# Part of the attention matrix transposed by TensorE instead of by DMA

## The chip, the cores and the metric

The kernel runs on one core of one Trainium2 chip. The core has a matrix engine (TensorE, PE in the profile, with its weight loads listed as PEld), three elementwise engines (VectorE or DVE, ScalarE or ACT, GpSimd or POOL), a queue engine (SyncE or SP) that issues most transfers, and 16 DMA engines. The metric is the time of one execution on the device in microseconds, as the median of several runs.

## What is computed

One transformer block over a sequence of 2048 rows of 1024 float32 values:

```python
u   = rms_norm(h, norm1_w);  proj = u @ w_in        # [diff q,k,v | sb q,k,v]
y_diff = diff_attention(dq, dk, dv, lam, rel_bias)  # 4 heads, softmax
# stick breaking, 8 heads, no softmax, strictly causal:
z = q @ k.T * scale
log_1mb = where(mask, log_sigmoid(-z), 0)
rem = cumsum(log_1mb, axis=keys, reverse=True) - log_1mb
a = where(mask, exp(log_sigmoid(z) + rem), 0);  y_sb = a @ v
h = h + concat(rms_norm(y_diff), rms_norm(y_sb)) @ w_out
h = h + (silu(u2 @ w_gate) * (u2 @ w_up)) @ w_down  # u2 = rms_norm(h, norm2_w)
```

The change concerns the product of the stick-breaking weights `a` with `v`. TensorE contracts over partitions, so `a`, which is made with queries on partitions and keys along the row, has to be transposed first: blocks of 128 queries by 128 keys, keys onto partitions.

To keep float32 accuracy with 16-bit operands, a float32 value is split into a high float16 part and a low one (the value less the high part). A product then takes three matmuls: high by high, high by low, low by high.

## The kernel before

The work falls into eight head groups and then the output projection and the feed-forward part. Groups 0 to 3 are one differential head each (`diff_attn`); groups 4 to 7 are two stick-breaking heads each (`sb_attn`). While a group's attention runs, the projection of the next group is issued in small pieces between its units: `advance` follows the share of the group's work that is done. So TensorE has projection matmuls (L341) to do in between. Groups 4 to 6 are the "turned" ones, whose q and k come out of the projection already transposed (`proj_turned`, `turned_out`).

Within a group of `sb_attn` the loop runs over 16 query blocks `i`, over key ranges `b` of up to 1024 keys from the last to the first, and over the two heads `m`. One turn of it is a unit. For `i` from 0 to 7 there is one range of 128 to 1024 keys; for `i` from 8 to 15 there is a range of 128 to 1024 keys and then one of 1024. That gives 48 units in a group. Of these, 16 have 512 keys or fewer: eight at the start of the group (`i` from 0 to 3) and eight in its middle (`b` = 1, `i` from 8 to 11), where they alternate with units of 1024.

`stage_a` makes a unit's weights. For each chunk of up to 512 keys TensorE writes the scores into a PSUM tile `sc` (L506, and L508 for the mask). ACT applies two sigmoids to it (L618, L619), DVE runs the product scan along the row (L621), and DVE, or POOL for the first half of a wide unit, multiplies (L622). The result stands in the float32 tile `be`. `split_t` then makes the high part on ACT (a cast in the helper on L89), the low part on POOL (a subtraction in the helper on L98), both into a 16-bit tile `s16`, and one DMA transpose on SP's queue (L460) turns both parts into the tile `aT`. After a delay of `lag` units (7, and 5 in group 6) `stage_b` issues the matmuls with `v` (L517).

Tiles come from rings: four `sc` tiles in PSUM, nine `z4` tiles (each unit takes two, `be` and `om`), three `s16` tiles, six `aT` tiles. In groups 4 and 5 a counter `wide` sends some units to borrowed tiles for `s16` and `aT` (two of five, and one of four). A new tile waits until the last reader of the one that it replaces is done.

Every engine works through its own queue in a fixed order, which is set when the program is built: a planner orders the instructions by priorities (`PRI`, with `at` for `stage_a` above the rest and `pm` for the projection below) and by its own estimate of when they are ready. Inside `tc.issue_after(x)`, instructions on x's engine are put behind x. `pick` gives an operation to the engine with the lower sum of booked costs, `note` books a cost, and `level` resets the sums at every fourth query block.

Of the kernel before, what the change touches and what calls it, by code (L numbers as in the profile page):

```python
# [11 lines left out]
F32 = mybir.dt.float32  # L12
F16 = mybir.dt.float16
# [3 lines left out]
ALU = mybir.AluOpType  # L17
# [4 lines left out]
S, D, P = 2048, 1024, 128  # L22
# [16 lines left out]
QB, KB, ZB, AB, SB, PD = 4, 7, 9, 6, 3, 5  # L39
# [20 lines left out]
def block(tc, a, out):  # L60
    nc = tc.nc
    PE, ACT, DVE, POOL, SP = nc.tensor, nc.scalar, nc.vector, nc.gpsimd, nc.sync
    top = ExitStack()
    with top:
# [8 lines left out]
        def note(e, ns):  # L73
            load[e] += ns * KW[e]
# [6 lines left out]
        def level():  # L81
            for k in load:
                load[k] = 0.0

        def to16(dst, src, n, engines="ADP", psum=False):
            cost = {"A": 0.84 * n + 110, "D": (1.05 if psum else 0.53) * n + 70, "P": 1.1 * n + 80}
            e = pick(**{k: cost[k] for k in engines})
            if e == "A":
                ACT.copy(dst, src)  # L89
            elif e == "D":  # L90
                DVE.tensor_copy(dst, src)
            else:
                POOL.tensor_scalar(dst, src, 1.0, 0.0, op0=ALU.mult, op1=ALU.add)

        def tt(dst, a_, b_, op, n, engines="DP"):
            cost = {"D": 1.15 * n + 70, "P": 2.45 * n + 80}
            e = pick(**{k: cost[k] for k in engines})
            (DVE if e == "D" else POOL).tensor_tensor(dst, a_, b_, op)  # L98

        def pri(k):  # L100
            def deco(f):
                @functools.wraps(f)
                def g(*args):
                    with tc.high_priority(PRI[k]) if PRI[k] else nullcontext():
                        return f(*args)
                return g
            return deco

        def nm(s):
            uid[0] += 1  # L110
            return f"{s}{uid[0]}"
# [5 lines left out]
        id32 = cp.tile([P, P], F32, name="id32")  # L117
# [138 lines left out]
        with ExitStack() as ph1:  # L256
            sp = ph1.enter_context(tc.tile_pool(name="sp", bufs=2))
            ps = ph1.enter_context(tc.tile_pool(name="ps", bufs=2, space=PSUM))
# [4 lines left out]
            def z4():  # L263
                return zp.tile([P, 1028], F32, tag="z4", bufs=ZB, name=nm("z4"))
# [64 lines left out]
            def turned(g):  # L329
                return 4 <= g < NG - 1  # L330
# [117 lines left out]
            @pri("spl")  # L448
            def split_t(src, n, he="ADP", le="DP", wide=None):
                if wide is not None and wide % 5 in (1, 3):  # L450
                    s16 = pp.tile([P, 4, 256], F32, tag="raw", name=nm("s16"))[:].rearrange("p t n -> p (t n)").bitcast(F16)
                else:
                    s16 = s16p.tile([P, 2048], F16, tag="s16", bufs=SB, name=nm("s16"))
                to16(s16[:, :n], src, n, he)
                tt(s16[:, n : 2 * n], src, s16[:, :n], ALU.subtract, n, le)
                if wide is not None and wide % 4 == 3:
                    aT = pp.tile([P, 4, 4, 2, 64], F16, tag="st", name=nm("aT"))[:].rearrange("p c t s e -> p (c t) (s e)")
                else:
                    aT = sp.tile([P, 16, P], F16, tag="aT", bufs=AB, name=nm("aT"))
                SP.dma_start_transpose(aT[:, : 2 * n // P, :], s16[:, : 2 * n])  # L460
                return aT
# [36 lines left out]
            def fq(g, i):  # L498
                k = 2 if g == NG - 1 else 4
                return (i % k, k)  # L500

            @pri("sc")
            def score_chunk(G, sc, i, q, m, w, cut=False, turned=False):
                terms = ((m, 0), (2 + m, 0), (m, 1)) if turned else ((2 + m, m), (m, m))
                for o, (a_, b_) in enumerate(terms):
                    last = PE.matmul(sc[:, : 128 * w].rearrange("p (t n) -> p t n", n=P), lhsT=G["q"][i // 4][:, a_, i % 4, :], rhs=G["k"][q][:, b_, 0:w, :], start=o == 0, stop=o == len(terms) - 1)  # L506
                if cut:
                    last = PE.matmul(sc[:, 128 * w - P : 128 * w], lhsT=idb[:], rhs=tri[:], start=False, stop=True, skip_group_check=True)  # L508
                return last.ins
# [85 lines left out]
            def sb_attn(g, G):  # L595
                last = {}
                front = []
                wide = [0]
                lag = PD + 2 if g < NG - 2 else PD

                @pri("at")
                def stage_a(i, m, b):
                    L = (i + 1) * 128
                    n = min(1024, L - 1024 * b)
                    be, om = z4(), z4()
                    if b == i // 8:
                        DVE.memset(om[:, n : n + 1], 8192.0)
                    else:
                        DVE.tensor_copy(om[:, n : n + 1], last[m][:, 0:1])
                    last[m] = om  # L610
                    for c in range((n - 1) // 512, -1, -1):
                        lo, hi = 512 * c, min(512 * c + 512, n)
                        w = hi - lo
                        sc = ps.tile([P, 512], F32, tag="sc", bufs=4, name=nm("sc"))
                        front.append(score_chunk(G, sc, i, 2 * b + c, m, w // P, b == i // 8 and hi == n, turned(g)))
                        aside = c == 1 and turned(g)
                        beta = be[:, lo:hi] if aside else sc[:, :w]
                        ACT.activation(om[:, lo:hi], sc[:, :w], AF.Sigmoid, scale=G["nkz"][:])  # L618
                        ACT.activation(beta, sc[:, :w], AF.Sigmoid, scale=G["kz"][:])  # L619
                        ov = om[:, lo:hi][:, ::-1]  # L620
                        DVE.tensor_tensor_scan(ov, ov, sc[:, :w], om[:, hi : hi + 1], op0=ALU.mult, op1=ALU.bypass)  # L621
                        (POOL if aside else DVE).tensor_tensor(be[:, lo:hi], beta, om[:, lo + 1 : hi + 1], ALU.mult)  # L622
                        note("A", 1.7 * w + 400)
                        note("D", 2.1 * w + 150)
                        note("P" if aside else "D", (1.65 if aside else 1.05) * w + 100)
                    wide[0] += 1
                    return n, split_t(be[:, :n], n, "A", "P", wide[0] if g < NG - 2 else None)

                ypd = {}

                def stage_b(i, m, b, n, aT):
                    with tc.issue_after(front[-1]):
                        stage_c(i, m, b, n, aT)

                def stage_c(i, m, b, n, aT):
                    r, k = fq(g, i)
                    if i // k not in ypd:
                        ypd[i // k] = ps.tile([P, 512], F32, tag="yp", name=nm("yp"))
                    yp = ypd[i // k]
                    pv(G, yp, P * r + 64 * m, aT, b, n, 128 * m, 64, r == 0 and m == 0 and b == i // 8, r == k - 1 and m == 1 and b == 0)  # L640
                    if m == 1 and b == 0 and r == k - 1:
                        finish(g, G, i, k, yp)
                        G["fin"] = i + 1

                pend = []
                done = 0
                for i in range(NT):
                    if i % 4 == 0:
                        level()
                    for b in range(i // 8, -1, -1):  # L650
                        for m in range(2):
                            n, aT = stage_a(i, m, b)
                            pend.append((i, m, b, n, aT))
                            if len(pend) > lag:
                                stage_b(*pend.pop(0))
                            done += n // P + CS
                            yield done / (272 + 48 * CS), (i + 1 if b == 0 and m == 1 else i)
                for u in pend:
                    stage_b(*u)

# [212 lines left out]
        with ExitStack() as ph2:  # L873
# [23 lines left out]
            turn = [0]  # L897
# [400 lines left out]
```

## Time and profile before

| | us |
|---|---|
| median of 3 runs (2699.47 to 2701.21) | 2699.54 |
| the profiled execution, whole | 2702.93 |
| its span, first to last instruction | 2701.0 |
| stick-breaking groups 4 to 6 in it | about 612 to 1100 |
| DVE busy, whole span | 1959.8 (73%) |
| PE busy, whole span | 2508.6 (93%) |

The profile is one execution. Busy time of an engine is the union of its instructions' times; matmuls are pipelined, so four that take 0.27 us each can be done 0.6 us after the first began. A row of a group gives line, engine, operation, output and inputs by the program's names, shapes, count, busy time, mean time of one in ns, and after the bar the idle time of the engine before these instructions and what ended it. A row of a timeline gives start, length, engine and line, and in brackets the idle time before it and what ended that. A row of a window gives from-to, length, then the busy time of each engine with its count of instructions, the granted TensorE clock as a share of full speed, the DMA share and the rate in GB/s. A wait reads "who waited <- for what: total us, times, longest".

### The profile page before, as it was taken

To read this page: it belongs to the slowest core of one execution; us is meant where nothing else is said; L and a number is where in the kernel's file an instruction comes from. 1 tells how busy PE (TensorE), PEld (TensorE's weight loads), DVE (VectorE), ACT (ScalarE), POOL (GpSimd) and SP (SyncE) were. 2 spreads that over 40 slices of the span, in tenths; PEclk is the share of its full clock that TensorE was granted. 3 is DMA by queue.
4 is the path that set the end of the run, shared out by engine and by line. 5 is a ranking of instruction groups with operands and counts; after the bars stand their busy time and mean duration, and the time that the engine had idled before them with its cause. 6 is when DMAs were issued, how large, how long until landed. Compare 5 with 4: busy or idle time off the path is not lost. (4 is left out here: it accounts for less than half of the span.)

```text
span 2701.0 us, 50505 instructions
## 1 busy us (share of the span) xinstructions
PE 2508.6 (93%) x19628; PEld 1507.6 (56%) x19628; DVE 1959.8 (73%) x3712; ACT 1344.7 (50%) x2487; POOL 1517.8 (56%) x1097
## 2 busy tenths in 40 slices
PE   7998989899988989889999999999999999999999
PEld 4655656577776776567774444444444444444444
DVE  6898879899989889887866877778685543433434
ACT  4665656567978878765634534435352112111121
POOL 2578767768767767545665755665564332322323
PEclk9999999999999999999999999999999999999999
DMA  6778697768989989997996566565748744635532
GB/s 221 211 163 184 143 200 172 172 145 183 195 175 185 178 166 206 208 205 203 230 317 232 211 232 219 207 239 183 253 171 330 304 159 157 234 132 184 202 110 94
DMA packets 619584, 534.40 MB, mean 198 GB/s; under 512 B 480640, under 2 KB 548224, under 8 KB 609104
## 3 DMA queue, kind: packets, MB, share of 16 engines
q1 hardware_dynamic: 617520, 529.09, 70.1%
q8 instruction: 154, 2.52, 0.4%
q0 software_dynamic: 512, 1.36, 0.2%
q14 instruction: 86, 0.70, 0.1%
q10 hardware_dynamic: 1312, 0.72, 0.1%
HBM read 261.08 MB, written 147.32 MB: 151 GB/s over the span
## 5 line engine op out<-in xcount | busy, mean ns | idle before, releaser
L98 POOL TENSOR_TENSOR s<-z,s 128x1024 f16<-128x1024 f32 (+7 forms) x288 | 471.5, 1646 | 141.8 <-ACT s L89 118.2
L506 PE MATMUL sc<-kT,qT 128*128 128x512 f16 (+3 forms) x1520 | 382.7, 354 | 51.1 <-DVE z L622 18.6
L1104 PE MATMUL pd<-wd,act 128*128 128x512 f16 x1764 | 392.8, 380 | 5.3 <-DVE cu L1038 4.7
L621 DVE TENSOR_TENSOR_SCAN z<-z,sc 128x512 f32<-128x512 f32 (+3 forms) x320 | 352.8, 1112 | 56.5 <-ACT sc L619 34.6
L325 PE MATMUL pj<-w,xt 128*128 128x384 f16 x1920 | 354.6, 333 | 17.1 <-ACT raw L374 5.8
L1004 PEld LDWEIGHTS <-wu 128*128 128x128 f16 x1848 | 181.9, 98 | 224.6 <-issue 12.8
L1004 PEld LDWEIGHTS <-wg 128*128 128x128 f16 x1848 | 181.3, 98 | 222.9 <-issue 9.3
L517 PE MATMUL yp<-v,aT 128*128 128x64 f16 (+1 forms) x4896 | 271.2, 205 | 36.9 <-DMA aT<-s 35.7
L517 PEld LDWEIGHTS <-aT 128*128 128x128 f16 x4896 | 239.1, 100 | 114.4 <-DMA aT<-s 46.7
L98 POOL TENSOR_TENSOR act<-cg,act 128x512 f16<-128x512 f32 x109 | 150.7, 1393 | 259.4 <-ACT act L1063 259.4
L1104 PEld LDWEIGHTS <-act 128*128 128x128 f16 x1764 | 172.9, 98 | 213.5 <-issue 7.2
L325 PEld LDWEIGHTS <-xt 128*128 128x128 f16 x1920 | 187.8, 99 | 147.2 <-issue 23.4
L89 ACT CAST s<-z 128x128 f16<-128x128 f32 (+7 forms) x215 | 173.3, 810 | 135.9 <-DMA aT<-s 44.6
L98 POOL TENSOR_TENSOR stages<-stages 128x512 f32<-128x512 f32 x97 | 171.4, 1767 | 116.5 <-DVE wg L220 42.2
L618 ACT ACTIVATE z<-sc,c 128x512 f32<-128x512 f32 (+3 forms) x320 | 211.2, 665 | 24.4 <-PE sc L506 12.4
L98 POOL TENSOR_TENSOR hs<-hs,cu 128x512 f32<-128x512 f32 x102 | 133.6, 1317 | 159.3 <-DVE hs L1110 59.7
L506 PEld LDWEIGHTS <-qT 128*128 128x128 f16 x1520 | 128.8, 99 | 119.7 <-issue 23.9
L831 PE MATMUL po<-wo,mt 128*128 128x256 f16 x1536 | 182.4, 279 | 12.6 <-DVE xf L834 8.6
L1063 ACT CAST act<-cg 128x512 f16<-128x512 f32 x126 | 76.7, 616 | 231.1 <-DVE cg L1069 192.7
L1110 DVE SCALAR_TENSOR_TENSOR hs<-pd,c,hs 128x512 f32<-128x512 f32 x144 | 106.0, 747 | 115.0 <-PE pd L1104 105.3
L341 PE MATMUL pj<-xt,w 128*128 128x128 f16 x2304 | 177.4, 222 | 6.2 <-DVE v L363 5.2
L1004 PE MATMUL pm<-X,wu 128*128 128x512 f16 x792 | 179.8, 381 | 2.1 <-ACT cg L1049 1.7
(254 smaller groups left out, 4812.3 us busy)
## 6 DMA issues: line engine op xcount, KB each, us to landing
xt<-xs SPq DMA_DIRECT2D x112, 512.0 KB, 4.5
hs<-hd SPq DMA_DIRECT2D x72, 512.0 KB, 4.5
hd<-hs SPq DMA_DIRECT2D x56, 512.0 KB, 5.9
split<-wg SPq DMA_DIRECT2D x11, 1792.0 KB, 6.9
split<-wu SPq DMA_DIRECT2D x11, 1792.0 KB, 6.7
split<-wd SPq DMA_DIRECT2D x11, 1792.0 KB, 6.8
wg<-split SPq DMA_DIRECT2D x11, 1792.0 KB, 7.5
wd<-split SPq DMA_DIRECT2D x11, 1792.0 KB, 9.0
```

Of the source, the lines that this page charges most:

```text
L89: ACT.copy(dst, src)
L98: (DVE if e == "D" else POOL).tensor_tensor(dst, a_, b_, op)
L325: PE.matmul(pj[:, :384], lhsT=xv[:, xi, kt, :], rhs=G["w"][:, wi, kt, :], start=n == 0, stop=n == 23)
L341: PE.matmul(o, lhsT=x_ if c == 2 else w_, rhs=w_ if c == 2 else x_, start=n == 0, stop=n == 23)
L506: last = PE.matmul(sc[:, : 128 * w].rearrange("p (t n) -> p t n", n=P), lhsT=G["q"][i // 4][:, a_, i % 4, :], rhs=G["k"][q][:, b_, 0:w, :] ...
L517: PE.matmul(yp[:, y0 : y0 + wd], lhsT=aT[:, a_, :], rhs=v[:, v_ : v_ + wd], start=start and j == 0 and q == 0, stop=stop and j == nb - 1 a ...
L618: ACT.activation(om[:, lo:hi], sc[:, :w], AF.Sigmoid, scale=G["nkz"][:])
L621: DVE.tensor_tensor_scan(ov, ov, sc[:, :w], om[:, hi : hi + 1], op0=ALU.mult, op1=ALU.bypass)
L831: PE.matmul(po[:, sl], lhsT=mt[:, kt, P * xi : P * xi + P], rhs=wos[2 * h + n][wi][:, kt, :], start=q == 0, stop=q == 23)
L1004: PE.matmul(ps_[:].rearrange("p (t n) -> p t n", n=P), lhsT=wv[:, wo, wi, 128 * kt : 128 * kt + 128], rhs=X[xo][:, :, xi, kt, :], start=st ...
L1104: PE.matmul(po[:], lhsT=act[:, ao, xi, 128 * j : 128 * j + 128], rhs=W["d"][:, wo, wi, :], start=start and u == 0 and q == 0, stop=u == nu ...
L1110: DVE.scalar_tensor_tensor(dst, po[:], kd[:], src, op0=ALU.mult, op1=ALU.add)
```

## The change

In groups 4 to 6 a unit of at most 512 keys no longer goes through `split_t`. `stage_a` hands on its float32 tile `be`, and three units later `turn` is called for it, behind the last score matmul issued so far. `turn` takes one `sc` tile of PSUM, transposes each block of 128 keys in float32 on TensorE (a matmul with the identity `id32`), copies the result as float16 into the high half of an `aT` tile on ACT, and subtracts that from the PSUM tile on DVE into the low half. Units above 512 keys keep the DMA transpose; the counter `wide` counts only these now. `note` books the new ACT and DVE costs.

```diff
+                    if direct(n):
+                        return n, be
                     wide[0] += 1
                     return n, split_t(be[:, :n], n, "A", "P", wide[0] if g < NG - 2 else None)
+
+                def direct(n):
+                    return turned(g) and n <= 512
+
+                @pri("spl")
+                def turn(be, n):
+                    nb = n // P
+                    tr = ps.tile([P, 512], F32, tag="sc", bufs=4, name=nm("at"))
+                    for j in range(nb):
+                        PE.transpose(tr[:, P * j : P * j + P], be[:, P * j : P * j + P], id32[:])
+                    aT = sp.tile([P, 16, P], F16, tag="aT", bufs=AB, name=nm("aT"))
+                    src = tr[:, :n].rearrange("p (c n) -> p c n", n=P)
+                    ACT.copy(aT[:, :nb, :], src)
+                    DVE.tensor_tensor(aT[:, nb : 2 * nb, :], src, aT[:, :nb, :], ALU.subtract)
+                    note("A", 0.84 * n + 110)
+                    note("D", 1.15 * n + 70)
+                    return aT
+
+                def turn_due(n):
+                    u = pend[-n] if len(pend) >= n else None
+                    if u is not None and direct(u[3]):
+                        with tc.issue_after(front[-1]):
+                            u[4] = turn(u[4], u[3])
...
-                            pend.append((i, m, b, n, aT))
+                            pend.append([i, m, b, n, aT])
+                            turn_due(4)
...
+                for n in range(min(3, len(pend)), 0, -1):
+                    turn_due(n)
                 for u in pend:
                     stage_b(*u)
```

## Prediction

> **What bounds the kernel now.** The page comes first, for the span, then the busy time of each engine in stretches of the stage that the change touches, then that stage's waits. All threshold talk below uses 0.2% (5.4 us), about what a measurement of this kernel tells from no change.
>
> ```profile
> span 2701.0 us, 50505 instructions
> ...
> PE 2508.6 (93%) x19628; PEld 1507.6 (56%) x19628; DVE 1959.8 (73%) x3712; ACT 1344.7 (50%) x2487; POOL 1517.8 (56%) x1097
> ```
>
> The 73% of DVE is a mean over unlike stages. Cut into the stretches of groups 4 to 6:
>
> ```profile
> core 0: us, PE busy (x) PEld busy (x) DVE busy (x) ACT busy (x) POOL busy (x), PEclk, DMA share, GB/s
> 612.00:638.00 26.00, 25.04 (x392) 22.36 (x390) 22.98 (x48) 20.12 (x53) 18.67 (x20) 1.00 0.80 172
> 638.00:666.00 28.00, 23.52 (x348) 18.64 (x347) 27.55 (x57) 22.24 (x43) 23.50 (x15) 1.00 0.84 171
> 666.00:707.00 41.00, 36.32 (x559) 28.32 (x558) 38.18 (x61) 35.90 (x66) 31.27 (x25) 1.00 1.09 208
> 707.00:766.00 59.00, 55.17 (x898) 44.28 (x896) 56.37 (x87) 55.30 (x93) 46.79 (x34) 1.00 0.98 184
> 766.00:790.00 24.00, 21.29 (x335) 18.15 (x333) 17.90 (x41) 16.90 (x38) 13.56 (x15) 0.93 0.90 163
> 790.00:826.00 36.00, 30.58 (x463) 24.85 (x462) 31.61 (x62) 26.97 (x52) 25.95 (x17) 1.00 0.79 167
> 826.00:866.00 40.00, 35.45 (x554) 28.11 (x550) 38.17 (x62) 32.77 (x58) 28.49 (x23) 1.00 1.05 209
> 866.00:926.00 60.00, 56.06 (x912) 44.93 (x909) 57.29 (x92) 56.63 (x97) 49.47 (x35) 1.00 1.01 186
> 926.00:948.00 22.00, 19.22 (x292) 16.20 (x290) 17.30 (x37) 15.92 (x36) 11.14 (x13) 0.92 0.87 161
> 948.00:980.00 32.00, 25.49 (x385) 20.48 (x383) 25.16 (x53) 22.39 (x42) 23.55 (x17) 0.95 0.89 179
> 980.00:1030.00 50.00, 46.23 (x733) 38.61 (x730) 44.22 (x73) 38.00 (x70) 28.82 (x24) 0.97 0.81 155
> 1030.00:1100.00 70.00, 62.86 (x663) 39.64 (x661) 65.87 (x114) 58.90 (x104) 55.01 (x38) 1.00 1.02 229
> sum 488.00, PE 437.23 PEld 344.55 DVE 442.61 ACT 402.03 POOL 356.24; mean PE 36.44 PEld 28.71 DVE 36.88 ACT 33.50 POOL 29.69
> ```
>
> Each group has four stretches: its start (612, 766, 926; the first eight small units), a stretch of larger units, its middle (666, 826, 980; the other eight small units between units of 1024), and the rest. DVE is busy 442.6 of 488 us (90.7%), PE 437.2. In the middles of groups 4 and 5 DVE has 93 and 95%, so DVE sets the pace there. The starts are different: in the second and third DVE is at 75 and 79%, and nothing is full. The waits say why.
>
> ```profile
> ACT s L89 <- DMA aT<-s: 20.1, 13, 3.0
> ...
> PE sc L506 <- DVE z L622: 13.4, 19, 1.6
> ...
> DVE z L621 <- ACT sc L619: 11.7, 18, 2.7
> DVE z L621 <- ACT z L619: 11.2, 9, 4.0
> ...
> PE yp L517 <- DMA aT<-s: 10.0, 11, 2.1
> ```
>
> ACT waits 20.1 us until a transpose has left its `s16` tile, and PE 10.0 us for a transposed tile. At the start of group 5, in the timelines of ACT, DVE and PE:
>
> ```profile
> 772.65 0.30 ACT L89 CAST s<-z 128x128 f16<-128x128 f32 x1 [2.88 <-DMA aT<-s]
> 780.23 0.82 ACT L89 CAST s<-z 128x256 f16<-128x256 f32 x2 [3.04 <-DMA aT<-s]
> 773.90 1.01 DVE L621 TENSOR_TENSOR_SCAN z<-z,sc 128x384 f32<-128x384 f32 x1 [1.85 <-ACT sc L619]
> 782.22 1.28 DVE L621 TENSOR_TENSOR_SCAN z<-z,sc 128x512 f32<-128x512 f32 x1 [2.69 <-ACT sc L619]
> 772.67 1.29 PE L517 MATMUL yp<-v,aT 128*128 128x64 f16 x24 [2.15 <-DMA aT<-s]
> 773.77 2.00 PE L341 MATMUL pj<-xt,w 128*128 128x128 f16 x17
> ```
>
> ACT stands behind a small unit's cast, the next unit's sigmoids stand behind ACT, and DVE loses 1.85 and 2.69 us. PE waits 2.15 us for a unit of 24 matmuls (8 blocks by 3, a wide one of group 4), and runs slowly afterwards (17 matmuls in 2.00 us).
>
> **The change part by part.** In each of the six small-unit stretches eight units change, two of each of 128, 256, 384 and 512 keys: 20 blocks. In all 48 units, 120 blocks. Durations:
>
> ```profile
> 665.68 0.61 PE L488 MATMUL yp<-id,y 128*128 128x128 f32 x4
> L683 DVE TENSOR_TENSOR xt<-xtr,xt 128x512 f16<-128x512 f32 x32 | 21.1, 681 | 4.2 <-ACT xt L682 4.2
> L682 ACT CAST xt<-xtr 128x512 f16<-128x512 f32 x32 | 17.7, 586 | 7.3 <-PE xtr L664 6.7 <-ACT raw L374 0.5
> L622 DVE TENSOR_TENSOR z<-sc,z 128x384 f32<-128x384 f32 x12 | 6.7, 555 | 0.5
> L622 DVE TENSOR_TENSOR z<-sc,z 128x256 f32<-128x256 f32 x12 | 5.0, 420 | 1.0 <-POOL s L98 0.5
> L622 DVE TENSOR_TENSOR z<-sc,z 128x128 f32<-128x128 f32 x14 | 3.9, 282 | 0.3
> L89 ACT CAST s<-z 128x512 f16<-128x512 f32 x12 | 7.4, 631 | 0.7 <-DMA aT<-s 0.4 <-DVE z L607 0.3
> L98 POOL TENSOR_TENSOR s<-z,s 128x512 f16<-128x512 f32 x12 | 13.9, 1161 | 1.2 <-ACT s L89 1.2
> L460 SPq DMA_TRANSPOSE aT<-s x288: 1167/1556/5872, 113.7 to 1358.9; - x144
> L362 DVE TENSOR_SCALAR kT<-pj 128x256 f16<-128x256 f32 x20 | 8.3, 413 | 0.0
> L362 DVE TENSOR_SCALAR v<-pj 128x256 f16<-128x256 f32 x15 | 6.1, 408 | 0.6 <-PE pj L341 0.5
> L349 ACT ACTIVATE qT<-pj,half 128x256 f16<-128x256 f32 x42 | 21.8, 519 | 11.2 <-PE pj L341 7.9 <-DVE qT L350 3.2
> ```
>
> *DVE, added.* The subtraction out of PSUM is L683 at 512 keys; shorter ones are taken from L622, which also reads PSUM. Per stretch 2 x (0.282 + 0.420 + 0.555 + 0.681) = 3.88 us, in all 23.3.
>
> *DVE, moved.* The booked DVE cost pushes `pick` towards ACT. Two ACT instructions of L349 come with two picks, so the 42 there mean 42 picks, of which DVE took 20 + 15. The six stretches last 203 of 488 us and hold some 14.6 of these 35; I let two thirds, about 10, go over: 10 x 0.41 = 4.0 us, 0.66 per stretch (ends: none, and all 6.0). ACT's room takes them. Net DVE 3.2 per stretch, 19.3 in all.
>
> *PE, added.* Four float32 transposes end 0.61 us after the first began, and one takes 0.27, so one follows another after 0.11: 20 x 0.11 = 2.2 us per stretch, 13.2 in all. Where DVE sets the pace, PE's idle time covers this (36.32 of 41 busy); at 612 it does not.
>
> *ACT.* Cast for copy, 631 against 586 ns: nothing.
>
> *POOL, removed.* At most 48 x 1.16 = 56 us; POOL is busy 356 of 488 and not the bound of any stretch: nothing directly.
>
> *SP and the DMA engines, removed.* 48 issues of median 1.56 us, 75 us of SP's queue; the wide units' transposes and the loads of `xt` behind them are issued earlier. The gain is what ended in DVE's idle time: between 0 and the 20.1 + 10.0 us of waits shown (a loss is excluded: fewer transfers queue ahead). I count 4.5 us at 766 (both DVE stalls) and half of the 4.7 idle at 926, where the same cause stands beside others; at 612 nothing, since PE is full (25.04 of 26). The wait of PE for the wide unit stays.
>
> *Rings.* The transposed tile takes one of four `sc` tiles, so scores run ahead by less; `be` is held three units longer out of nine `z4`. Cost from 0 (fewer buffers cannot help) to 48 x (0.586 + 0.681) = 61 us, were no score to start while a transposed tile is emptied. Queue order: ACT's copy and DVE's subtraction stand in front of the next sigmoids and scans, so a late transpose makes ACT late. I take 0, as the nearest row, PE's 13.4 us of waiting for score tiles, is mostly DVE being full, and give the rest to a rival.
>
> **The sum**, DVE's net 3.2 per stretch less what is freed or idle. Starts: 612, PE's +2.2; 766, 3.2 - 4.5 = -1.3; 926, 3.2 - 2.3 = +0.9. Middles: a third of the idle 2.82, 1.83 and 5.78 takes some up: 3.2 - 0.9, 3.2 - 0.6, 3.2 - 1.9 = +2.3, +2.6, +1.3. Together +8.0 us. The profiled execution (2702.9 with the 1.9 around its span) would become 2710.9; it is 3.4 above the median, which becomes 2707.5.
>
> **The rivals.** Break-even is handy: DVE must do 442.6 + 19.3 = 461.9 us, so the change gains if DVE's share in this stage rises from 90.7 above 461.9 / 488 = 94.7%. My forecast is 461.9 / 496 = 93.1%.
>
> *A, faster: the transposes were the bound.* If the wait for them is what holds ACT, all starts close up, and POOL's relief lets ACT's casts of wide units go sooner. For: stretches with no small units reach 56.37 / 59 = 95.5% and even 27.55 / 28 = 98.4%; the clock at 766 and 926 was 0.93 and 0.92. At 95.5% the stage takes 483.6 (-4.4), at 98.4% 469 (-19); I take a value between, nearer the first as wide stretches are commonest at 95%, -9: 2690.5. Against: 948 (79%) has no small unit and is slow too. It decides from 94.7% up.
>
> *B, much slower: the score ring.* If each of the 48 units delays the scores by a quarter of the 1.27 us, that is 15 on top of 8: 2722.5. For: PE already waits on L622. Against: the planner can delay the transposes.
>
> *C, nothing to see.* The added DVE work falls wholly in the 24.2 us of DVE idle of the six stretches: 0 to +3, 2701.
>
> *D, the clock.* The granted clock falls when TensorE has little to do, as at 766. Were the transposes to count as such and hold 0.93 in all six stretches, 203 x 0.07 = 14 us on top of 8: 2721. Against: the four float32 transposes at 665.68 (L488) lie between two stretches with clock 1.00. The Trainium skill, "TensorE: Matmul & The Clock Gate", Part 4, states that transposes do not count as busy for the clock in the usual way, and that one takes about 275 ns in a kernel; the 0.27 agrees, but at 275 each the added PE time would be an estimated 33 us, where the row's spacing gives 13.2.
>
> **How the numbers follow.** Forecast 0.45 (+3 to +16; 0.12 of it within 0.2%, 0.33 above); A 0.30 (-3 to -19; 0.03 within, 0.27 below); B 0.13; C 0.08; D 0.04. So faster 0.27, same 0.12 + 0.03 + 0.08 = 0.23, slower 0.50. The likeliest gives 2707.5, alone 2702 to 2716. The range reaches into A to -14.5 and through B and D to +28.5: 2685 to 2728, leaving out A's far end and B's.
>
> **What would show it.** Right: 48 fewer transposes; the L89 waits on DMA at the starts gone; DVE busy in the stage up by about 19, its share near 93%; fewer L362 on DVE; the middles longer by about 2 each. Wrong: DVE's share above 94.7% (A); PE's waits for L622 or for the new subtraction well above 13.4 (B); the clock below 1.00 in the middles (D).

## The result, and the profile after

The changed kernel takes 2732.11 us (median of 4 runs, 2726.8 to 2734.45), the kernel before, on the same chip, 2699.51 (2699.16 to 2701.21): 1.0117 times as long, with a 95% interval of 1.0101 to 1.0133. It is slower by 32.6 us, where the forecast was 8, and outside the range, which ended at 2728.

The profiled execution took 2726.8 us, the fastest of its four; that of before had been 3.4 above its median. So the two traces differ by 24.0 us of span, and only this much can be followed in them. From the page of the changed kernel:

```profile
span 2725.0 us, 50599 instructions
...
PE 2516.5 (92%) x19748; PEld 1518.1 (56%) x19748; DVE 1975.2 (72%) x3749; ACT 1349.9 (50%) x2498; POOL 1480.0 (54%) x1049
```

From here on "the stage" runs from the first product scan of group 4 to the first of group 7, so that the same work is compared whatever its place in the span. In the table of windows, before, the row of the stage, then three stretches: the query blocks 4 to 7 of group 4 (no small units), the small units in the middle of group 4, and the start of group 5.

```profile
605.80:1095.10 489.30, 440.08 (x6545) 348.38 (x6543) 442.95 (x769) 402.81 (x737) 357.41 (x267) 0.98 0.94 186
...
630.90:659.60 28.70, 24.43 (x361) 19.37 (x359) 28.02 (x53) 25.70 (x56) 22.29 (x19) 1.00 0.80 151
...
659.60:707.50 47.90, 42.66 (x659) 33.77 (x656) 44.74 (x76) 40.04 (x73) 38.05 (x28) 1.00 1.07 211
...
765.00:784.80 19.80, 17.65 (x299) 15.47 (x295) 13.92 (x34) 12.11 (x29) 10.79 (x11) 0.91 0.95 173
```

The same four in the changed kernel:

```profile
602.50:1113.80 511.30, 455.26 (x6687) 362.81 (x6684) 460.76 (x817) 409.50 (x749) 320.86 (x220) 0.99 0.79 166
...
629.70:665.80 36.10, 28.64 (x421) 23.49 (x420) 35.22 (x63) 26.26 (x51) 21.51 (x18) 1.00 0.66 148
...
665.80:718.70 52.90, 48.07 (x745) 39.44 (x742) 46.40 (x84) 44.80 (x82) 29.57 (x19) 1.00 0.81 169
...
776.00:797.60 21.60, 18.27 (x297) 16.32 (x295) 15.37 (x40) 11.27 (x25) 6.22 (x4) 0.92 0.63 128
```

The stage is 22.0 us longer, 24.0 less 2.0 that lie elsewhere (3.3 less ahead of it, 1.1 more in group 7, 4.2 more behind the last scan). DVE works 17.8 us more in it (460.76 - 442.95) and is idle 4.2 more (50.54 against 46.35): its share goes from 90.5% to 90.1%. Length by stretch, after less before, from such windows:

| group | start (small units) | blocks 4 to 7 | middle (small and wide) | blocks 12 to 15 |
|---|---|---|---|---|
| 4 | +2.1 | +7.4 | +5.0 | -0.2 |
| 5 | +1.8 | +2.0 | +1.6 | +0.6 |
| 6 | +1.1 | -2.9 | +3.0 | +0.5 |

Groups of the changed kernel by line, with count and min/median/max in ns:

```profile
L643 DVE TENSOR_TENSOR aT<-at,aT x48: 264/476/692, 621.5 to 1054.4; 128x128 f16<-128x128 f32 x12, 128x256 f16<-128x256 f32 x12, 128x384 f16<-128x384 f32 x12, 128x512 f16<-128x512 f32 x12
...
L362 DVE TENSOR_SCALAR kT<-pj x17: 394/415/417, 638.1 to 1008.8; 128x256 f16<-128x256 f32 x17
L362 DVE TENSOR_SCALAR v<-pj x17: 266/393/425, 657.6 to 1121.4; 128x256 f16<-128x256 f32 x9, 128x128 f16<-128x128 f32 x8
...
L639 PE MATMUL at<-id,z x120: 272/273/456, 607.9 to 1048.0; 128*128 128x128 f32 x120
...
L460 SPq DMA_TRANSPOSE aT<-s x240: 1169/1616/5276, 113.8 to 1378.8; - x120
```

The 48 subtractions cost 22.0 us (by length 3.0, 4.7, 6.3 and 8.0); of the 35 projection parts of 256 columns that DVE had, 17 + 9 are left, and 9 x 0.41 = 3.7 us went to ACT; 48 DMA transposes are gone. What DVE waits for has changed. Waits of the changed kernel from 602 to 1122 us:

```profile
DVE z L621 <- ACT sc L619: 24.9, 30, 3.2
ACT z L618 <- PE sc L506: 23.1, 30, 2.1
...
PE sc L506 <- DVE z L621: 15.8, 18, 2.9
ACT z L618 <- PE sc L508: 14.8, 13, 2.9
PE sc L506 <- DVE z L622: 14.1, 14, 2.7
...
PE yp L517 <- DMA aT<-s: 8.6, 6, 3.2
ACT aT L642 <- PE at L639: 8.2, 4, 4.2
...
DVE z L621 <- ACT z L619: 4.7, 9, 0.8
...
PE pj L341 <- DVE v L363: 5.6, 4, 1.9
```

And those of the kernel before in the same span of time that have changed or are needed below:

```profile
ACT z L618 <- PE sc L506: 6.5, 6, 2.2
ACT z L618 <- PE sc L508: 5.7, 4, 4.4
PE pj L341 <- DVE v L363: 5.2, 6, 2.3
PE sc L506 <- DVE z L621: 4.4, 11, 0.9
```

ACT no longer waits for DMA (24.3 us in this span before, 1.1 now). It waits for scores instead: 37.9 us against 12.2. DVE's scans wait 24.9 us for the sigmoids that L619 writes into `sc`, against 11.7, but only 4.7 for those that it writes into `z` (the first half of a wide unit), against 11.2. Together that is 29.6 us against 22.9: of ACT's 25.7 us more of waiting for scores, 6.7 reach DVE. The start of group 5, where the prediction had two stalls disappear, shows one such place. From the timelines of PE, ACT and DVE there, in the changed kernel:

```profile
784.05 1.46 PE L517 MATMUL yp<-v,aT 128*128 128x64 f16 x24 [3.25 <-DMA aT<-s]
785.33 0.46 PE L639 MATMUL at<-id,z 128*128 128x128 f32 x1
785.58 2.79 PE L341 MATMUL pj<-xt,w 128*128 128x128 f16 x36
788.20 0.19 PE L517 MATMUL yp<-v,aT 128*128 128x64 f16 x1
788.23 0.65 PE L506 MATMUL sc<-kT,qT 128*128 128x384 f16 x3
...
793.12 0.50 PE L639 MATMUL at<-id,z 128*128 128x128 f32 x3
...
785.82 0.27 ACT L642 CAST aT<-at 128x128 f16<-128x128 f32 x1 [4.17 <-PE at L639]
789.03 0.58 ACT L618 ACTIVATE z<-sc,c 128x384 f32<-128x384 f32 x1 [2.95 <-PE sc L508]
...
786.12 0.29 DVE L643 TENSOR_TENSOR aT<-at,aT 128x128 f16<-128x128 f32 x1 [1.37 <-ACT aT L642]
...
790.09 1.01 DVE L621 TENSOR_TENSOR_SCAN z<-z,sc 128x384 f32<-128x384 f32 x1 [3.21 <-ACT sc L619]
```

PE stands 3.25 us at a wide unit's product, whose tile still comes by DMA. The small unit's transpose stands behind it on PE, ACT's copy waits 4.17 us for that, and the next scores come 4.2 us after the wait ended (784.05 to 788.23), behind 36 projection matmuls. DVE loses 1.37 + 3.21 = 4.58 us, against the 1.85 + 2.69 = 4.54 that were to be saved. That the two sums agree so closely is chance. ACT's wait for the DMA went; PE's, 2.15 us at a product of the same size before, stayed, and ACT now waits behind it.

### The profile page after: what moved, and what is told of

Same layout as the page of the kernel before. It is cut to its first block, busy times and chain, and to the rows that moved or that the text cites. A ratio compares the mean times of both kernels' runs of the same rounds, so it can differ in the third digit from the quotient of the medians.

```text
span 2725.0 us, 50599 instructions
## 1 busy us (share of the span) xinstructions
PE 2516.5 (92%) x19748; PEld 1518.1 (56%) x19748; DVE 1975.2 (72%) x3749; ACT 1349.9 (50%) x2498; POOL 1480.0 (54%) x1049
## 5 line engine op out<-in xcount | busy, mean ns | idle before, releaser
L98 POOL TENSOR_TENSOR s<-z,s 128x1024 f16<-128x1024 f32 (+7 forms) x240 | 431.2, 1804 | 105.6 <-ACT s L89 81.3
L506 PE MATMUL sc<-kT,qT 128*128 128x512 f16 (+3 forms) x1520 | 382.2, 353 | 62.6 <-DVE z L622 17.8
L621 DVE TENSOR_TENSOR_SCAN z<-z,sc 128x512 f32<-128x512 f32 (+3 forms) x320 | 354.7, 1113 | 54.7 <-ACT sc L619 41.6
L325 PE MATMUL pj<-w,xt 128*128 128x384 f16 x1920 | 356.5, 334 | 15.5 <-ACT raw L374 5.8
L618 ACT ACTIVATE z<-sc,c 128x512 f32<-128x512 f32 (+3 forms) x320 | 205.4, 642 | 44.2 <-PE sc L506 25.6
L89 ACT CAST s<-z 128x1024 f16<-128x1024 f32 (+6 forms) x167 | 148.6, 891 | 128.4 <-issue 34.4
L1032 PE MATMUL pm<-X,wg 128*128 128x512 f16 x792 | 178.9, 379 | 0.0
```

The source lines that it names most:

```text
L325: PE.matmul(pj[:, :384], lhsT=xv[:, xi, kt, :], rhs=G["w"][:, wi, kt, :], start=n == 0, stop=n == 23)
L1032: PE.matmul(ps_[:].rearrange("p (t n) -> p t n", n=P), lhsT=wv[:, wo, wi, 128 * kt : 128 * kt + 128], rhs=X[xo][:, :, xi, kt, :], start=st ...
```

## The experiments

Four explanations stood against one another: the DVE work of the subtraction; the score ring (rival B); the bookings, which send projection parts from DVE to ACT; and the order of the queues, which the planner works out anew when anything changes. The expectations name them by letters or words of their own. For each run the row of the stage is the measure: before, DVE is busy 442.95 of 489.30 us and idle 46.4; after, 460.76 of 511.30 and idle 50.5. Where the end of the stage misleads, because group 7 gives back or adds to what the stage lost, the time from the first scan of group 4 to the last of group 7 stands beside it: 747.1 us before, 770.2 after.

**The subtraction alone.** The kernel before, with the same subtraction for the same 48 units, but in SBUF and into a tile that nobody reads, and with its booking:

```diff
+                if extra:
+                    scr = s16p.tile([P, 512], F16, tag="scr", bufs=1, name=nm("scr"))
+                    DVE.tensor_tensor(scr[:, :n], src, s16[:, :n], ALU.subtract)
+                    note("D", 1.15 * n + 70)
```

> The kernel before, with DMA transposes everywhere, plus one DVE subtraction of the same size for each of the 48 small units of groups 4 to 6 (into a scratch tile, booked with the planner as in the change). Theory DVE bill (the stage gets longer because DVE, its pace-setter, gets some 19 us more and nothing takes it up): 15 to 25 us above before. Theory score ring (the transposed tile takes score tiles of PSUM and makes PE and ACT late): nothing here touches PSUM, so less than 8 us above before.

Ratio 1.0113 (1.0098 to 1.0128), 2729.97 us. The row of the stage:

```profile
602.40:1124.10 521.70, 451.00 (x6554) 356.45 (x6551) 467.18 (x806) 408.68 (x752) 362.18 (x268) 0.95 0.84 176
```

DVE works 24.2 us more, idles 8.2 more, and the stage is 32.4 longer. The time is as much longer as with the whole change, but neither the price nor the wait is the same. Out of SBUF the times of these 48 subtractions add up to 35.2 us (more than DVE's busy time grew), where the change's out of PSUM add up to 22.0, and PE's projection waits for the low parts from DVE 20.1 us, against 5.2 before and 5.6 after. So this run does not price the change's subtraction.

**The transposes alone.** The kernel before with its DMA path, and beside it the transposes of the small units into `sc` tiles, of which ACT reads one column per block; no work on DVE:

```diff
+                def turn(be, n):
+                    tr = ps.tile([P, 512], F32, tag="sc", bufs=4, name=nm("at"))
+                    for j in range(n // P):
+                        PE.transpose(tr[:, P * j : P * j + P], be[:, P * j : P * j + P], id32[:])
+                    scr = s16p.tile([P, 8], F32, tag="scr", bufs=1, name=nm("scr"))
+                    ACT.copy(scr[:, : n // P], tr[:, :n].rearrange("p (c n) -> p c n", n=P)[:, :, 0])
```

> The kernel before, DMA transposes kept, plus the 120 float32 transposes of TensorE into score tiles three units later, as in the change; the tile is given back by a copy of one column per block on ACT, and its result is not used. Theory DVE bill: within 5 us of before (PE's 13 us lie in its idle time). Theory score ring: 10 us or more above before, with ACT waiting for scores well above the 12 us that it waits before.

Ratio 1.0087 (1.006 to 1.0114), 2722.15 us.

```profile
599.80:1102.90 503.10, 453.38 (x6690) 363.38 (x6687) 443.95 (x771) 408.77 (x787) 361.30 (x269) 0.98 0.87 182
```

With DVE's work unchanged the stage is 13.8 us longer, nearly all of it DVE idle time (59.2). The scans' waits in the stage:

```profile
DVE z L621 <- ACT sc L619: 22.4, 28, 2.8
DVE z L621 <- ACT z L619: 12.7, 12, 3.4
```

That is 35.1 us of waiting for the sigmoids, against 22.0 before and 28.9 after in the stage, though ACT itself waits only 18.5 us for scores (12.2 before). From the first scan of group 4 to the last of group 7 the kernel takes 755.8 us, 8.7 more than before, as group 7 gives 5.1 back. Behind the last scan it takes another 13.9 us more than before (1362.0 against 1348.1), for which no cause was found.

**The change without the subtraction.** POOL writes zeros into the low half, so the low part of the small units is left out:

```diff
-                    DVE.tensor_tensor(aT[:, nb : 2 * nb, :], src, aT[:, :nb, :], ALU.subtract)
+                    POOL.tensor_scalar(aT[:, nb : 2 * nb, :], aT[:, :nb, :], 0.0, 0.0, op0=ALU.mult, op1=ALU.add)
...
-                    note("D", 1.15 * n + 70)
```

> The changed kernel without the DVE subtraction: POOL writes zeros as the low half instead, so the low part of the small units is left out. Theory DVE bill: the 23 us of subtractions go and the gain of fewer DMA transposes is left, so -8 to +5 us against before. Theory score ring: the PSUM tile is freed only some 0.5 us earlier for each unit, so 10 to 25 us above before remain.

Ratio 1.0053 (1.0036 to 1.0069), 2713.58 us.

```profile
602.40:1109.70 507.30, 459.07 (x6678) 364.19 (x6677) 446.51 (x779) 404.50 (x737) 341.27 (x267) 0.97 0.75 166
```

DVE is back to within 3.6 us of its old work, but the stage only to within 18.0: DVE idles 60.8. The scans' waits in the stage:

```profile
DVE z L621 <- ACT sc L619: 35.4, 38, 2.1
DVE z L621 <- ACT z L619: 3.9, 7, 1.7
```

That is 39.3 us, and ACT waits 34.1 for scores. Beside this kernel the subtraction and its booking behave in the stage as the prediction thought: 14.3 us more work for DVE, of which 10.3 fall into idle time. But that idle time was not there before the change. By the medians the two are worth more: this kernel is 15.5 us slower than before, where the changed one is 32.6. Of these 17 us the traces hold 11.8, only 4.0 of them in the stage (4.2 in group 7, 3.5 behind the last scan), and no run tells why.

**Another ring.** The transposed tile comes from the ring of the products `yp` instead of the scores' (`tag="yp"` in place of `tag="sc", bufs=4`).

> The changed kernel with the transposed tile taken from the other PSUM ring (yp, two tiles) and not from the four score tiles. Theory DVE bill: no change against the changed kernel, 25 to 33 us above before. Theory score ring: at least 10 us of the 32 come back, and ACT's waits for scores fall to about those of before.

Ratio 1.0068 (1.0053 to 1.0083), 2717.13 us.

```profile
599.30:1110.00 510.70, 453.38 (x6710) 362.28 (x6707) 457.87 (x811) 408.95 (x754) 321.11 (x221) 0.98 0.80 165
```

The kernel is 19.0 us slower than before, where the changed one is 32.6, but the stage is as long as in the changed kernel. Within it, group 4 is only 4.4 us longer than before, against 14.3 with the score ring, and its scans wait 1.7 us for the sigmoid that L619 writes into `sc`, against 8.2; groups 5 and 6 take that away again (+17.0, against +7.7). So the score ring costs some 10 us in group 4. Whether it does so in the other two this run can't say, since there PE's transposes wait as well, 3.3 us, for a `yp` tile that L643 still reads. What makes the whole kernel shorter than the changed one lies in group 7 (249.5 us, against 258.9), where neither kernel has such transposes, so it can't be credited to the ring. Over the whole stage the scans wait 21.8 us for the sigmoids, as before (22.0), while ACT still waits 32.8 for scores: that wait by itself is not a loss to DVE.

**One place at a time.** The change for the starts alone (`i < 4` added to the condition in `direct`), and for the middles alone (`i >= 8`):

> The change in the first eight units of groups 4 to 6 alone (24 units). Theory DVE bill: half of the DVE work, less the DMA stalls at the starts, 5 to 14 us above before. Theory score ring: 8 to 16. Theory plan: nearly all of the 32 us or anything between 10 and 30, so that this run and the next sum to well above 32.

> The change in the eight middle units of groups 4 to 6 alone (24 units). Theory DVE bill: the dearer half, 12 to 20 us above before. Theory score ring: 12 to 20. Theory plan: anything between 10 and 30, the sum with the other half well above 32.

The starts: 1.004 (1.0026 to 1.0055), 2710.96 us, stage 502.8. The middles: 1.0097 (1.0082 to 1.0112), 2725.5 us, stage 506.8. Neither place gains. Their stages are 13.5 and 17.5 us longer, 31 together, where both at once cost 22.0: the parts don't add up.

**Bookings, and almost no work.** To the kernel before, for the same 48 units, first the booking alone with no instruction, then a copy of a single column on DVE with no booking:

```diff
+                    if turned(g) and n <= 512:
+                        note("D", 1.15 * n + 70)
```

```diff
+                    if turned(g) and n <= 512:
+                        scr = s16p.tile([P, 8], F32, tag="scr", bufs=1, name=nm("scr"))
+                        DVE.tensor_copy(scr[:, :1], be[:, :1])
```

> The kernel before with nothing but the change's booking of DVE cost for the 48 small units, without any added instruction; some high-part instructions move from DVE to ACT. Theories DVE bill and score ring: 0 to -5 us against before. Theory plan: 8 us or more above before.

> The kernel before plus, for each of the 48 small units, a DVE copy of a single column into a scratch tile (some 3 to 7 us of DVE in all, nothing booked); its only weight is that the planner orders the queues anew. Theories DVE bill and score ring: 3 to 7 us above before at most. Theory plan (the order of the queues before is a lucky one for this program, and any edit in these units makes the planner write another, in which scores come later): 10 to 25 us above before, with ACT's waits for scores near 25 us and not 12.

The booking alone: 1.0158 (1.0143 to 1.0173), 2742.2 us, more than the change. The single column: 1.005 (1.0032 to 1.0069), 2714.78 us, stage 504.5 with DVE busy 449.9. The row of the stage and two waits in it, booking alone:

```profile
599.70:1127.50 527.80, 453.01 (x6598) 360.39 (x6596) 443.08 (x763) 408.23 (x750) 360.73 (x269) 0.95 0.83 174
```

```profile
PE pj L341 <- DVE v L363: 18.5, 6, 4.5
PE sc L506 <- DVE kT L362: 14.6, 5, 4.9
```

DVE is busy as long as before (443.08) and idles 38.4 us more. Nine projection parts of 256 columns went to ACT, as in the changed kernel; the order was rewritten, and PE now stands 33.1 us at projection results of DVE, against 5.4 before. The copies of one column show a smaller form of it (9.9 + 5.9).

**The change without its booking on DVE** (`note("D", ...)` taken out of `turn`, the subtraction kept):

> The changed kernel without the booking of the subtraction on DVE (the line note of D with 1.15 per key); the subtraction itself stays, so the output is the reference's. Theory W (the subtraction's own DVE work is the loss): the picks stay on DVE, DVE busy in groups 4 to 6 rises by another 3 to 4 us over the changed kernel's 460.8, and the time stays at or a little above it, ratio to before 1.011 to 1.014. Theory B (the booking, which sends projection parts from DVE to ACT, is what costs): the time falls by much of the +38 us of idle that the bookings alone brought, ratio 1.000 to 1.006, with DVE idle in the stage falling from 50 to 46 or less.

Ratio 1.0104 (1.0073 to 1.0135), 2729.73 us; stage 511.8, DVE busy 463.85. The projection parts are back on DVE and nothing is gained. So what the bookings cost alone is not what they cost here.

**One instruction.** Into both kernels, one DVE memset of a column at the start of group 4 (d0), or one ACT copy of a column in its block 6 (p6), to make the planner write another order:

> The kernel before plus one single DVE instruction (a memset of one column of a scratch tile) in the first unit of group 4. Theory that the change's own work costs the 32 us: within 2 us of before. Theory plan: the order of all later queues is drawn anew, 5 to 25 us above before.

> The kernel before plus one single ACT instruction (a copy of one column) in a unit of query block 6 of group 4, a second draw of the order. Own work: within 2 us of before. Plan: 5 to 25 us above before, and not the same as the first draw.

> The changed kernel plus the same one DVE instruction in the first unit of group 4. Own work: within 3 us of the changed kernel (32 above before). Plan: anywhere from 10 to 45 us above before; if the DVE bill is paid on top of the draw, the mean of the changed kernel's draws lies 15 to 20 us above the mean of the draws of before.

> The changed kernel plus the same one ACT instruction in query block 6 of group 4. Own work: within 3 us of the changed kernel. Plan: anywhere from 10 to 45 us above before.

Only a few instructions changed places, so these say nothing of the order; they are repeats. Ratios 1.0 and 0.9998 (both within 0.998 to 1.0016) for the kernel before, 1.0122 (1.0105 to 1.0138) and 1.0125 (1.0096 to 1.0154) for the changed one. The stage is 490.1 and 490.9, and 512.8 and 514.5. They also show where the rest of the 32.6 us can lie: from the last scan to the end they take 1347.2 and 1344.4 us before, 1356.0 and 1354.0 after, 9 us apart, where the first pair of traces had 4.2. What causes it was not found, and it need not belong to the change: in the pair with `fin` below it is the other way round (1352.6 before, 1348.6 after).

**Another order with the same work.** In both kernels, one class of work gets priority 1 instead of 0: `po`, the splitting of the projection's results, and, in a run of its own, `fin`, the finishing of a query block's output:

```diff
-PRI = {"sc": 0, "spl": 0, "pv": 0, "fin": 0, "pm": -200, "po": 0, ...}
+PRI = {"sc": 0, "spl": 0, "pv": 0, "fin": 0, "pm": -200, "po": 1, ...}
```

> The kernel before with the priority of one class of work, the one named po, raised from 0 to 1 and nothing else: the same instructions, possibly in another order on the queues. Theory O (the order of before is a favourable one and any redrawn order costs idle time): if instructions are moved within groups 4 to 6, DVE idle rises from 46.4 to 54 or more and the ratio is 1.003 or more; if none are moved there, the ratio is 0.999 to 1.001. Theory W: within 1.002 either way.

> The changed kernel with the same priority raised from 0 to 1. Theory O: with instructions moved in groups 4 to 6 the time differs from the changed kernel's by several us to either side (ratio to before anywhere from 1.004 to 1.020); with none moved it is 1.010 to 1.014. Theory W: 1.010 to 1.014 either way.

> The kernel before with the priority of the class named fin raised from 0 to 1 and nothing else; the order of the queues then differs from the first stick-breaking group on and not ahead of it, and no instruction is added or removed. Theory O (the order of before is a favourable one, and any other costs DVE idle time): DVE busy in groups 4 to 6 at 443 to 446, idle above 54, ratio 1.004 to 1.018. Theory W (work alone counts; the other redrawn orders were bad luck of larger redraws): idle 46 to 50, ratio 0.998 to 1.003.

> The changed kernel with the same priority raised from 0 to 1, again with another order from the first stick-breaking group on. Theory O: a draw from the same spread as the kernel before with a redrawn order, so the ratio to before is 1.004 to 1.018 and may lie below that of the run beside it. Theory W: DVE busy 458 to 462 and the ratio 1.010 to 1.014, about 0.012 above the run beside it.

With `po`, the kernel before takes 1.0149 (1.0113 to 1.0185), 2737.73 us, and the changed one 1.0156 (1.0125 to 1.0187), 2742.07 us. With `fin`, 1.0046 (1.0028 to 1.0064), 2713.07 us, and 1.0106 (1.0087 to 1.0126), 2729.91 us. Stage of the kernel before with `po` at 1:

```profile
614.50:1125.90 511.40, 444.83 (x6558) 353.68 (x6556) 445.39 (x775) 406.29 (x743) 358.30 (x268) 0.96 0.88 181
```

With `fin` at 1:

```profile
608.00:1097.20 489.20, 435.50 (x6518) 343.33 (x6515) 443.26 (x770) 403.59 (x738) 357.31 (x267) 0.99 0.92 185
```

The changed kernel with `fin` at 1:

```profile
603.80:1115.00 511.20, 452.20 (x6664) 360.08 (x6661) 461.48 (x817) 409.32 (x750) 321.55 (x220) 0.99 0.78 165
```

`fin` gives the same pair of stages in a slightly other order, 489.2 and 511.2: again +22.0, of it 18.2 work and 3.8 idle time. By the medians, though, the change costs only 16.8 us in this pair. `po` costs the kernel before as much as the change does, with no work added; there too PE waits for DVE's projection results (13.6 + 9.5 us). The changed kernel stays at 507.1 (457.62 busy) with `po`. So it is not true that any other order costs, as one theory had it; but one with the same work can cost 22 us in this stage.

**A way without work on DVE.** The split stays in SBUF on ACT and POOL; TensorE transposes both float16 halves into one PSUM tile of the score ring, and ACT alone copies it out. Here `turn` is called one unit later and not three:

```diff
+                        s16 = s16p.tile([P, 2048], F16, tag="s16", bufs=SB, name=nm("s16"))
+                        to16(s16[:, :n], be[:, :n], n, "A")
+                        tt(s16[:, n : 2 * n], be[:, :n], s16[:, :n], ALU.subtract, n, "P")
...
+                    tr = ps.tile([P, 1024], F16, tag="sc", bufs=4, name=nm("at"))
+                    for j in range(2 * nb):
+                        PE.transpose(tr[:, P * j : P * j + P], be[:, P * j : P * j + P], id16[:])
...
+                    ACT.copy(aT[:, : 2 * nb, :], tr[:, : 2 * n].rearrange("p (c n) -> p c n", n=P))
```

> The changed kernel with the split left where it was, in SBUF on ACT and POOL, and both float16 halves then transposed by TensorE into one PSUM tile, which ACT alone copies out; nothing is subtracted or booked on DVE; the output is the reference's. Twice the transposes (240 in place of 120) and ACT copies of twice the length: from the 266/447/649 ns rows about 48 times 0.35 = 17 us more on ACT, which idles 102 us in the stage. Theory W (DVE's work is the loss): DVE busy in groups 4 to 6 is back at 443 to 447 and the ratio at 0.998 to 1.004. Theory O (every rewriting of the queues' order costs DVE idle time): DVE busy is back too, but its idle time is at 54 to 61 against 46.4 before, and the ratio is 1.004 to 1.008. If ACT's longer copies hold the score tiles: above 1.010.

Ratio 1.0251 (1.0219 to 1.0282), 2766.14 us, the slowest of all. DVE works 450.2 us in a stage of 542.3 and idles 92.1. Its scans wait for the sigmoids 62.7 us (39.6 and 23.1), and PE's transposes wait 12.9 us for ACT's casts. So taking the work off DVE in this way made the chain through PE and ACT in front of DVE slower; how much of that the shorter delay does was not tried.

The stage of the kernels beside one another, in us. "Projection" is what PE's L341 waits for the low part of v on DVE (L363) and PE's scores for the high part of k on DVE (L362):

| kernel | stage | DVE busy | DVE idle | scans for sigmoids | ACT for scores | PE for projection |
|---|---|---|---|---|---|---|
| before | 489.3 | 443.0 | 46.4 | 22.0 | 12.2 | 5.4 |
| changed | 511.3 | 460.8 | 50.5 | 28.9 | 35.4 | 5.6 |
| subtraction alone | 521.7 | 467.2 | 54.5 | 34.4 | 29.4 | 20.1 |
| transposes alone | 503.1 | 444.0 | 59.2 | 35.1 | 18.5 | 7.5 |
| changed, no subtraction | 507.3 | 446.5 | 60.8 | 39.3 | 34.1 | 4.4 |
| changed, other ring | 510.7 | 457.9 | 52.8 | 21.8 | 32.8 | 8.7 |
| booking alone | 527.8 | 443.1 | 84.7 | 49.1 | 39.8 | 33.1 |
| before, `po` at 1 | 511.4 | 445.4 | 66.0 | 42.7 | 26.7 | 23.1 |
| changed, `po` at 1 | 507.1 | 457.6 | 49.5 | 31.0 | 32.8 | 3.6 |

No variant was faster than the kernel before.

## Why the prediction was wrong, point by point

- **What bounds the stage.** Right: DVE sets its pace, at 90.5% and 90.1%. The break-even at a share of 94.7% was never near, and the forecast of 93.1% did not come.
- **DVE added and moved.** Right: 22.0 against 23.3 us, 3.7 against 4.0, and 17.8 against 19.3 net. Three of the eight subtractions of a start come after it, since `turn` runs three units late, so the starts were charged for work of the blocks 4 to 7. The +7.4 us there in group 4 are DVE work that also came from elsewhere (35.22 against 28.02 busy): the stretches of the sum were cut more finely than the planner keeps them.
- **PE.** Right: 13.2 us were forecast, and PE is busy 15.2 more in the stage (455.26 - 440.08). The Trainium skill's figure of about 275 ns for a transpose in a kernel, given for bfloat16 ("TensorE: Matmul & The Clock Gate", Part 4), agrees with the 273 ns of one in float32, not with the rate: three end 0.50 us after the first began (the row at 793.12), so one follows another after some 0.11, as the prediction had it.
- **The DMA waits.** Half right: they left ACT. But DVE's 4.5 us at group 5's start, which were to go, are 4.58 us of other stalls, because PE's wait for the wide unit, which the prediction itself left standing, now has a small unit's transpose and the next scores behind it. What is late next was not asked of PE's queue.
- **Rings and queue order, taken as 0, and the idle time that was to absorb the rest.** Here the sum failed. It let 11.3 of DVE's net 19.3 us be taken up by freed or idle time; the idle time rose by 4.2 instead. So the stage grew by 22.0 us and not by 8.0, which is 14.0 of the 24.6 us that the forecast lacks; 2.0 lie elsewhere in the traces, and 8.6 are not in them. The transposes without the subtraction lengthen the stage by 13.8 and by 18.0 us with DVE hardly busier. Those two kernels show few waits for projection results (7.5 and 4.4 us), so theirs is not the loss that `po` and the booking alone show; what grew in them is DVE's wait for the sigmoids (35.1 and 39.3 us, from 22.0). That the transposes' place in PE's and ACT's queues causes it is seen line by line at the start of group 5, and argued for the rest; a new order of the other instructions, which each of these kernels has too, is not ruled out as a part of it. The longer hold of `be` shows no wait of its own: nothing but ACT's copy waits for L639. The row that I leaned on, PE's 13.4 us for score tiles on L622, was the wrong one to price them by, for it stayed (14.1). The scores late at ACT, 37.9 us from 12.2, are no price either, as the run with the other ring shows.
- **Rival B**, the score ring at +23, had the direction, and part of the mechanism. Its sign as written did not come (PE's wait for L622 stayed, that for the subtraction is 1.1 us), but the wait of score tiles for L621 went from 4.4 to 15.8 us. With the other ring, PE's waits on L621 and L622 together fall to 17.8 us in the stage, from 28.5 in the changed kernel (16.7 before), and group 4 gets some 10 us back. Another ring alone doesn't shorten the stage, though, so the ring is not the whole cause. Its time, 2722.5, was still 9.6 us short.
- **Rival D**, the clock: wrong. The granted clock of the stage is 0.99 against 0.98; it is 1.00 in the middle of group 4, where small units are transposed, and 0.92 at the start of group 5, where it had been 0.91. Part 4 of that page of the Trainium skill states that transposes don't count as busy for the clock in the usual way; in clusters of up to four, between other matmuls, they lowered nothing here. Nor is the rival's first step, a lower clock where TensorE has little to do, borne out by the mean load: in the prediction's own rows PE is busy 84% of the stretch at 638 with the clock at 1.00, and 89% of that at 766 with 0.93.
- **Rivals A and C**: wrong. Faster transposes didn't close the starts, and the work didn't vanish in idle time.

What stays open: how much of the 22 us any pair of orders would show, and with it how much is the change's own. In the three pairs the change costs 32.6, 16.8 (`fin`) and 4.3 us (`po`) by the medians. The changed kernel's stage lies between 507 and 515 us in five orders and repeats; that of before lies at 489 to 491 in four, at 511.4 with `po` at 1, and at 527.8 with the booking alone. The 4.3 us stand against an order of before that has a loss of its own. The 8.6 us of the median that the two traces don't hold stay unexplained too.

## What to carry to other kernels

Before counting a removed stall as gain, look for the next engine that waits for the same late thing, and list what the change puts behind it on that engine's queue: at the start of group 5 the transfer stayed late for the wide unit, and TensorE, which waits for it, now holds up ACT's copy and the scores. Idle time of the bounding engine may only be counted as cover if the change doesn't touch the chain that causes it. Where a planner writes the queues, run both kernels with a changed order and no changed work before a difference of one per cent is put down to the work.

## What the runs showed that was not expected

- A booking with no instruction behind it cost 43 us (1.0158), and one step of one priority 36 us (1.0149) or 11 us (1.0046), with the same instructions on every engine but for what the booking moved from DVE to ACT.
- Two losses that look alike at DVE, as late sigmoids, differ further up: with the booking alone PE waits 33.1 us for DVE's projection results, from 5.4; in the changed kernel 5.6. ACT's waits for scores don't tell them apart, since they grew in both (39.8 and 35.4 us in the stage, from 12.2).
- The same subtraction takes DVE 0.28 to 0.68 us in the mean out of PSUM (128 to 512 keys, in the changed kernel) and 0.42 to 0.93 us out of SBUF (in the run with the subtraction alone), where single ones reach 2.1 us.
- The Trainium skill, "VectorE: DVE Perf Modes", Rules for kernel authors, advises TensorE for a transpose of 128 by 128 where a result in PSUM will do, and the DMA otherwise. This case agrees with the second half: the result had to leave PSUM again, 264 to 692 ns on DVE for each unit and a copy on ACT, and with the DMA transposes, issued at a median of 1.56 us on SP's queue, the kernel was 32.6 us faster.
